# Storing the middle blocks row by row, with a load between the two rows, in a softmax-minus-one-hot kernel

## The chip, the cores and the metric

The kernel runs on one core of one Trainium2 chip. The metric is the device time of one execution in microseconds, lower is better; a time is the median of several runs. A microsecond is written us.

## The reference, cut to what matters

The input is 8192 rows (8 x 1024) of 8192 float32 numbers each, and one label for each row. The result is the gradient of the cross entropy: the softmax of each row, less 1 at the label's place.

```python
batch, seq_len, vocab = 8, 1024, 8192
logits_max = np.max(logits, axis=-1, keepdims=True)
exp_logits = np.exp(logits - logits_max)
softmax = exp_logits / np.sum(exp_logits, axis=-1, keepdims=True)
one_hot[batch_idx, seq_idx, labels] = 1.0
return (softmax - one_hot).astype(np.float32)
```

256 MiB are read and 256 MiB are written; nothing is read twice.

## The kernel before

**Tiles.** The 8192 rows are cut into B = 32 blocks of 256 rows. A block lies on 128 partitions with G = 2 rows to a partition, so it has 8 MiB; "row 0" and "row 1" of a block below mean the 128 first and the 128 second rows of the partitions, 4 MiB each. On chip there is one buffer `X` with SLOTS = 3 places for whole blocks; block b uses place b % 3. The work is done in place: the load writes into the place, the exponentials and the result overwrite it, and the store reads it. So block b can be loaded only when the store of block b-3 has landed.

**The work on one block** (`work(b)`). VectorE (DVE) takes the maximum of row 0 (`row_max`), ScalarE (ACT) makes its exponentials and their sum (`exponentials`), DVE takes the maximum of row 1, ACT makes its exponentials, and then DVE finishes row 0 and row 1 (`finish`): a reciprocal of the sum, and one `scalar_tensor_tensor` that multiplies the row by it and subtracts the mark at the label. The marks lie in PSUM as bytes (`hot`) and are made by ACT ahead of time (`mark`, two activations a row). `finished[t]` is what a store waits for, t = 2b or 2b+1.

**The transfers.** All loads and stores are issued by SyncE (SP), one after another in one order that is written out by hand; SP does nothing else. If an instruction of SP has to wait, all that stand behind it wait too. They all go into one hardware queue (q1), which works them off in their order on 16 DMA engines, each engine with its share of every transfer. `LOADS` and `STORES` say with one letter for each block how it is moved: `w` is the whole block in one transfer of 8 MiB, `r` is two transfers of 4 MiB, row 0 and row 1. A store by rows waits for its own row alone; a whole store waits for `finished` of row 1. Loads of blocks 0 to 5 and 31 go by rows, those of 6 to 30 whole. The last block is stored in four quarters.

**The order.** The loads of blocks 0, 1 and 2 come first. Then, after the work of block b, its store is issued, and behind it the load of the next block that has not been loaded. After block EARLY = 3 there is no load, so that from block 4 on the load behind the store of block b is that of b+2 and not b+3: it needs the place of block b-1. After block LATE = 27 two loads (29 and 30) follow, so that block 31 is loaded behind the store of block 28. In the middle the order of SP is: store of 10, load of 12, store of 11, load of 13, and so on.

Where this text writes S(b) it means the store of block b and S(b,0), S(b,1) its rows; L(b) is the load of block b.

Of the kernel before, what the change touches and what calls it, by code (L numbers as in the profile page):

```python
# [9 lines left out]
SLOTS = 3  # L10
EARLY = 3
LATE = 27

LOADS = "rrrrrrwwwwwwwwwwwwwwwwwwwwwwwwwr"
STORES = "rrrwwwwwwwwwwwwwwwwwwwwwwwwwrrrr"


@with_exitstack
def kernel(
# [19 lines left out]
    B = T // G  # L39
# [25 lines left out]
    with tc.tile_critical():  # L65
# [6 lines left out]
        def run(engine, waits, counter, method, **operands):  # L72

            waits = list(dict.fromkeys(waits))
            for w in waits[:-1]:
                engine.wait_ge(*w)
            instruction = getattr(engine, method)(**operands)  # L77
            for w in waits[-1:]:
                instruction._wait_ge(*w)
            step = 16 if method == "dma_start" else 1  # L80
            instruction.then_inc(counter, step)
            count[counter.name] = count.get(counter.name, 0) + step
            return counter, count[counter.name]
# [9 lines left out]
        def meets(a, b):  # L93
            sets = [[set(range(*d.indices(n))) for d, n in zip(p, (P, G))] for p in (a, b)]
            return all(x & y for x, y in zip(*sets))
# [4 lines left out]
        def load(b):  # L100
            loaded[b] = []
            before = stored.get(b - SLOTS, [])
            for q, piece in enumerate(PIECES[LOADS[b]]):
                ps, js = piece
                free = [w for other, w in before if meets(piece, other)]
                w = run(
                    nc.sync, free, got[b % SLOTS][q], "dma_start",
                    out=X[ps, b % SLOTS, js, :], in_=x_b[b, ps, js, :],
                )
                loaded[b].append((piece, w))  # L110

        def store(b):
            stored[b] = []
            if b == B - 1:
                for t in (T - G, T - 1):
                    j = t % G
                    for i, cs in enumerate(sides):
                        w = run(
                            nc.sync, [sides_done[t][i]], put[b % SLOTS][G * j + i],
                            "dma_start", out=o_b[b, every, one[j], cs], in_=X[every, b % SLOTS, one[j], cs],  # L120
                        )
                        stored[b].append(((every, one[j]), w))
                return
            for q, piece in enumerate(PIECES[STORES[b]]):
                ps, js = piece
                w = run(
                    nc.sync, [finished[b * G + js.stop - 1]], put[b % SLOTS][q], "dma_start",
                    out=o_b[b, ps, js, :], in_=X[ps, b % SLOTS, js, :],
                )
                stored[b].append((piece, w))  # L130
# [106 lines left out]
        def work(b):  # L237
            t0, t1 = b * G, b * G + 1
            row_max(t0)
            exponentials(t0)  # L240
            if b == 0:
                mark(0)
                mark(1)
            row_max(t1)
            exponentials(t1)
            finish(t0)
            mark(t0 + G)
            finish(t1)
            mark(t1 + G)

        nxt = SLOTS
        for b in range(B):
            work(b)
            store(b)
            if b == EARLY:
                continue
            for _ in range(2 if b == LATE else 1):
                if nxt < B:
                    load(nxt)
                    nxt += 1  # L260
        for b in range(B - SLOTS, B):
            for _, w in stored[b]:
                nc.scalar.wait_ge(*w)
# [30 lines left out]
```

## Time and profile before

| what | before |
|---|---|
| median of 3 runs | 1263.8 us (1263.55 to 1264.0) |
| the profiled execution, its own time | 1262.39 us |
| its span, first to last instruction | 1260.6 us |
| DVE busy | 1120.2 us (89%) |
| ACT busy | 722.7 us (57%) |
| bytes moved | 536.99 MB, mean 426 GB/s over the span |

The span is read from the hardware profiler's record of one execution; the execution's own time is 1.8 us more than its span, and the median of the runs is 1.4 us more than that. Every instruction is issued through one helper, so all have one line (L77): groups are told apart by what they write and read ("X<-in_logits_dram" is a load, "out_dram<-X" a store, "m<-X" the row maximum, "X<-X,r,hot" the finish). Rows of the timeline begin with the start in us and the duration in us, "x2" says that two instructions were merged into one row, and the bracket at the end gives the idle time before and what ended it. A DMA instruction on "SPq" shows when SP issued the transfer, not when the data moved. Rows of a table by windows hold, for each stretch, the busy time of each engine, the granted TensorE clock, the share of the DMA engines and the GB/s.

### The profile page before, as it was taken

To read this page: it belongs to the slowest core of one execution; us is meant where nothing else is said; L and a number is where in the kernel's file an instruction comes from. 1 tells how busy PE (TensorE), PEld (TensorE's weight loads), DVE (VectorE), ACT (ScalarE), POOL (GpSimd) and SP (SyncE) were. 2 spreads that over 40 slices of the span, in tenths; PEclk is the share of its full clock that TensorE was granted. 3 is DMA by queue.
4 is the path that set the end of the run, shared out by engine and by line. 5 is a ranking of instruction groups with operands and counts; after the bars stand their busy time and mean duration, and the time that the engine had idled before them with its cause. 6 is when DMAs were issued, how large, how long until landed. Compare 5 with 4: busy or idle time off the path is not lost.

```text
span 1260.6 us, 747 instructions
## 1 busy us (share of the span) xinstructions
PE 0.4 (0%) x2; PEld 0.3 (0%) x2; DVE 1120.2 (89%) x208; ACT 722.7 (57%) x257; POOL 2.3 (0%) x7
## 2 busy tenths in 40 slices
PE   0000000000000000000000000000000000000000
PEld 0000000000000000000000000000000000000000
DVE  6899999688988889888898888988889888898995
ACT  3666676356655575545755547555475554755662
POOL 0000000000000000000000000000000000000000
DMA  9999999999999999999999999999999999999998
GB/s 401 416 433 433 434 448 433 430 433 430 433 430 433 433 420 416 430 433 433 416 443 406 433 433 433 412 420 433 433 433 401 430 433 433 433 433 400 435 432 368
DMA packets 11574, 536.99 MB, mean 426 GB/s; under 512 B 1296, under 2 KB 1296, under 8 KB 1328
## 3 DMA queue, kind: packets, MB, share of 16 engines
q1 hardware_dynamic: 11520, 536.88, 99.5%
q10 hardware_dynamic: 48, 0.07, 0.0%
q14 instruction: 6, 0.05, 0.0%
HBM read 268.50 MB, written 268.44 MB: 426 GB/s over the span
## 4 chain that ended last, share of the span: by engine, by line
DVE 50%; DMA 43%; issue 4%; ACT 2%; SPq 0%
DMA X<-in_logits_dram 43%; DVE X L77 25%; DVE m L77 25%; ACT X L77 1%; DVE r L77 1%; ACT hot L77 0%; SPq L77 0%; ACT away L77 0%; SPq L289 0%; SPq L65 0%
## 5 line engine op out<-in xcount | busy, mean ns | idle before, releaser
L77 DVE TENSOR_REDUCE m<-X 128x1 f32<-128x8192 f32 x64 | 553.0, 8680 | 114.3 <-DMA X<-in_logits_dram 114.3
L77 ACT ACTIVATE X<-X,m 128x8192 f32<-128x8192 f32 x64 | 455.8, 7122 | 308.6 <-DVE m L77 308.6
L77 DVE SCALAR_TENSOR_TENSOR X<-X,r,hot 128x8192 f32<-128x8192 f32 (+1 forms) x66 | 560.1, 8489 | 3.8 <-ACT hot L77 1.6
L77 ACT ACTIVATE away<-count,word 128x2048 bf16<-128x2048 int16 x64 | 128.1, 2001 | 199.1 <-DVE X L77 148.1
L77 ACT ACTIVATE hot<-away,unit,minus 128x2048 int32<-128x2048 bf16 x64 | 131.9, 2061 | 2.1
L77 DVE RECIPROCAL r<-s 128x1 f32<-128x1 f32 x64 | 9.9, 155 | 2.4 <-ACT X L77 2.4
L77 ACT ACTIVATION_READ_ACCUMULATOR X<-X,m 128x1 f32 x64 | 11.9, 186 | 0.0
L77 DVE CAST lab_f<-lab_raw 32x256 f32<-32x256 int32 x1 | 0.4, 372 | 4.9 <-DMA lab_raw<-in_labels_dram 4.9
L77 ACT ACT_TABLE_LOAD x1 | 1.3, 1283 | 3.2 <-POOL count L77 3.2
L77 POOL IOTA count<- 128x2048 int16 x1 | 1.8, 1823 | 0.0
L77 DVE TENSOR_TENSOR unit<-unit,part 128x64 f32<-128x64 f32 x3 | 0.7, 224 | 0.1
L77 DVE CAST lab<-hot 128x64 int32<-128x64 f32 x1 | 0.2, 225 | 0.5 <-PE hot L77 0.5
L77 DVE TENSOR_SCALAR part<-minus 128x64 f32<-128x64 f32 x3 | 0.6, 195 | 0.1
L77 PE MATMUL hot<-ident,lab_f 32*128 32x32 f32 x2 | 0.4, 302 | 5.3 <-DVE lab_f L77 5.3
L77 PEld LDWEIGHTS hot<-ident,lab_f 32*128 32x128 f32 x2 | 0.3, 196 | 5.3 <-DVE lab_f L77 5.3
L77 DVE TENSOR_SCALAR part<-lab 128x64 int32<-128x64 int32 x1 | 0.2, 196 | 0.0
L77 DVE TENSOR_SCALAR word<-part 128x64 f32<-128x64 int32 x1 | 0.2, 195 | 0.0
L77 DVE TENSOR_SCALAR lab<-lab 128x64 int32<-128x64 int32 x1 | 0.2, 195 | 0.0
L77 DVE CAST minus<-lab 128x64 f32<-128x64 int32 x1 | 0.2, 195 | 0.0
L77 DVE TENSOR_SCALAR unit<-minus 128x64 f32<-128x64 f32 x1 | 0.2, 195 | 0.0
L77 DVE TENSOR_SCALAR minus<-unit 128x64 f32<-128x64 f32 x1 | 0.2, 195 | 0.0
L77 POOL TENSOR_SCALAR_AFFINE_SELECT ident<-ident 32x32 f32<-32x32 f32 x1 | 0.2, 203 | 0.1
(5 smaller groups left out, 0.5 us busy)
## 6 DMA issues: line engine op xcount, KB each, us to landing
X<-in_logits_dram SPq DMA_DIRECT2D x14, 4096.0 KB, 19.4
out_dram<-X SPq DMA_DIRECT2D x12, 4096.0 KB, 29.5
out_dram<-X SPq DMA_DIRECT2D x4, 2048.0 KB, 12.2
out_dram<-X SPq DMA_DIRECT2D x25, 23.7
X<-in_logits_dram SPq DMA_DIRECT2D x25, 43.1
lab_raw<-in_labels_dram ACTq DMA_DIRECT2D x1, 64.0 KB, 4.0
```

Of the source, the lines that this page charges most:

```text
L77: instruction = getattr(engine, method)(**operands)
```

## The change

The middle blocks are stored by rows as well, and the load of block b+2 is issued between the two rows of block b, for b from 4 to 27. After block 27 one more load (30) follows the store. What each engine computes, and its order, stays.

```diff
-STORES = "rrrwwwwwwwwwwwwwwwwwwwwwwwwwrrrr"
+STORES = "rrrrrrrrrrrrrrrrrrrrrrrrrrrrrrrr"
...
-        def store(b):
+        def store(b, between):
             stored[b] = []
...
             for q, piece in enumerate(PIECES[STORES[b]]):
                 ps, js = piece
+                if js.start:
+                    between()
                 w = run(
                     nc.sync, [finished[b * G + js.stop - 1]], put[b % SLOTS][q], "dma_start",
                     out=o_b[b, ps, js, :], in_=X[ps, b % SLOTS, js, :],
                 )
...
-        nxt = SLOTS
+        ahead = iter(range(SLOTS, B))
+
+        def next_load():
+            for n in ahead:
+                load(n)
+                return
+
         for b in range(B):
             work(b)
-            store(b)
-            if b == EARLY:
-                continue
-            for _ in range(2 if b == LATE else 1):
-                if nxt < B:
-                    load(nxt)
-                    nxt += 1
+            middle = EARLY < b <= LATE
+            store(b, next_load if middle else lambda: None)
+            if b < EARLY or b >= LATE:
+                next_load()
```

In the changed kernel the order of SP in the middle is: S(10,0), L(12), S(10,1), S(11,0), L(13), S(11,1), and so on. Up to the load of block 5 nothing moves. Block 3 is stored by rows with no load behind it. At the end the order is S(27,0), L(29), S(27,1), L(30), S(28,0), S(28,1), and from there on as before.

## The prediction

> **What bounds the kernel now.** I read the page first: busy times, the 40 slices, the chain that ended last.
>
> ```profile
> span 1260.6 us, 747 instructions
> ...
> DVE  6899999688988889888898888988889888898995
> ...
> DMA  9999999999999999999999999999999999999998
> GB/s 401 416 433 433 434 448 433 430 433 430 433 430 433 433 420 416 430 433 433 416 443 406 433 433 433 412 420 433 433 433 401 430 433 433 433 433 400 435 432 368
> ...
> DVE 50%; DMA 43%; issue 4%; ACT 2%; SPq 0%
> ```
>
> DVE carries half of the chain and is busy most of the time, but the DMA engines are busy in every slice, the first too. The chain as a list, one cycle of the middle, and the DVE timeline of that block show how the two meet:
>
> ```profile
> 276.78 16.00 DVE m L77 x2
> ...
> 311.80 0.33 SPq L77
> 312.13 0.04 issue
> 312.18 42.87 DMA X<-in_logits_dram
> 355.08 16.00 DVE m L77 x2
> ```
>
> ```profile
> 294.17 8.75 DVE L77 SCALAR_TENSOR_TENSOR X<-X,r,hot 128x8192 f32<-128x8192 f32 x1
> ```
>
> A block starts on DVE when its load lands (276.78). Row 0 is finished at 294.17 + 8.75 = 302.92, 26.1 us later; the whole block at 311.80, 35.0 us later. Then its store and the load of two blocks on are issued. The table of waits for the middle (230 to 1142 us) says that DVE is the one that waits:
>
> ```profile
> DVE m L77 <- DMA X<-in_logits_dram: 108.7, 24, 10.1
> ```
>
> 108.7 us over 24 loads: 35 us of work in a cycle of more than 39. So DMA sets the pace, and the question is whether its engines move bytes as fast as they can. SP's timeline gives the cycle in two stretches:
>
> ```profile
> 72.27 10.57 SPq L77 DMA_DIRECT2D X<-in_logits_dram  x2
> ...
> 111.19 10.47 SPq L77 DMA_DIRECT2D X<-in_logits_dram  x2
> ...
> 150.29 10.24 SPq L77 DMA_DIRECT2D X<-in_logits_dram  x2
> ...
> 273.17 0.33 SPq L77 DMA_DIRECT2D out_dram<-X  x1
> ...
> 1098.40 0.33 SPq L77 DMA_DIRECT2D out_dram<-X  x1
> 1098.78 23.30 SPq L77 DMA_DIRECT2D X<-in_logits_dram  x2
> ```
>
> Early, L(3,0), L(4,0) and L(5,0) are issued when S(0,0), S(1,0) and S(2,0) have landed: two cycles of 16.8 MB in 150.29 - 72.27 = 78.02 us, 39.01 each, all in transfers of one row. In the middle, from S(6) at 273.17 to S(27) at 1098.40, 21 cycles take 825.23 us, 39.30 each, all in whole blocks. The stretch with the smaller transfers is the faster one by 0.29 us a cycle. The table by windows, whose counts of whole packets are rougher, points the same way (last column):
>
> ```profile
> 72.27:150.29 78.02, 0.00 (x0) 0.00 (x0) 77.84 (x15) 51.64 (x19) 0.00 (x0) 1.00 1.00 431
> 390.09:1098.40 708.31, 0.00 (x0) 0.00 (x0) 628.50 (x108) 405.98 (x144) 0.00 (x0) 1.00 1.00 426
> 1162.00:1254.00 92.00, 0.00 (x0) 0.00 (x0) 84.33 (x17) 49.11 (x18) 0.00 (x0) 1.00 1.00 431
> ```
>
> 431 GB/s at both ends of the kernel, where transfers go by rows, 426 in the long middle. What differs besides the size is how much still lies in the queue when a store joins it. Issue to landing of the stores, middle and early:
>
> ```profile
> L77 SPq DMA_DIRECT2D out_dram<-X x22: 332/332/333, 273.2 to 1098.4; - x22
> ...
> DMA to landing us min/median/max: 22.9/23.6/24.6
> ```
>
> ```profile
> L77 SPq DMA_DIRECT2D out_dram<-X x5: 344/431/432, 82.9 to 160.6; - x5
> ...
> DMA to landing us min/median/max: 28.3/32.8/38.3
> ```
>
> A whole store moves in about 39.01 / 2 = 19.5 us, so in the middle it had 3.4 to 5.1 us between its issue and its first byte, the time of starting and landing included. What starting and landing cost on an empty queue the first load of the kernel shows:
>
> ```profile
> 0.96 12.42 DMA X<-in_logits_dram
> ```
>
> 12.42 us for one row, against 39.01 / 4 = 9.75 of moving: 2.7. That leaves the queue 0.7 to 2.4 us from dry whenever a middle store joins it, and the engines do not finish their shares at the same moment, so those ahead are already short of work. Early, a row's store (9.75) took at least 28.3: 18 us lay ahead of it. I read the 0.29 us a cycle as the price of the store that comes just in time.
>
> **The change part by part.**
>
> *The store of row 0 comes earlier.* Call D the landing of L(b). S(b,0) waits for row 0 alone, D + 26.1. In the queue stand then L(b+1), which lands a cycle after L(b), at D + 39.0, and S(b-1,1) behind it, to D + 48.8. So S(b,0) has 22 us ahead of it where S(b) had 4.
>
> *The load between.* L(b+2) needs the place of block b-1, so SP waits until S(b-1,1) has landed, D + 48.8. Behind the waiting SP stands S(b,1), whose row is ready at D + 35.0: it is held back 14 us, but its turn in the queue is only after L(b+2), so nobody feels that. Who covers the wait is S(b,0): 9.75 us, less the 2.7 of landing and starting, about 7 us left. Were this cover gone, each cycle would lose up to 2.7. So the thinnest point of the queue goes from 0.7 to 2.4 us to about 7, and the cycle, by the early rows, from 39.30 to 39.01. Those early cycles have the same pattern (a load that waits for a row's store, one row's transfer as cover). The rate itself has a bound: L(31,0) and L(31,1) are issued on the landing of S(28,0) and S(28,1),
>
> ```profile
> 1172.12 10.01 SPq L77 DMA_DIRECT2D X<-in_logits_dram  x2
> ```
>
> and the merged row ends with the second issue (0.34 us), so one row's landing follows the other by 9.67 us: 38.7 a cycle with no loss at all. The gain per cycle lies between nothing and 0.6; I take 0.29. It is had by the cycles with L(6) to L(29), 24 of them: 24 x 0.29 = 7.0 us.
>
> *25 more transfers.* Stores of blocks 3 to 27 become two. On SP that is 25 issues of 0.33 us, hidden because SP only waits in between. In the queue the cost of a transfer's ends is in the 39.01 already, which has four transfers a cycle where the changed middle has three.
>
> *L(30).* Before, it was issued when S(27) had landed, with L(29) as its cover:
>
> ```profile
> 1121.74 0.34 SPq L77 DMA_DIRECT2D X<-in_logits_dram  x1
> ```
>
> Now S(27,1) stands directly before it, and L(30) waits for that very store. Nothing lies in the queue meanwhile; S(28,0) and S(28,1) stand behind SP's wait. The queue runs dry once: between 0.4 (SP's own 0.33 and 0.04 in the chain) and 2.7 us. I take 2.0, nearer to the first load, because landing and starting both lie bare here.
>
> *The start and the end.* L(6) stands before S(4,1) now and lands 9.75 us sooner:
>
> ```profile
> 238.16 17.28 DVE L77 TENSOR_REDUCE m<-X 128x1 f32<-128x8192 f32 x2 [10.11 <-DMA X<-in_logits_dram]
> ...
> 1237.64 8.87 DVE L77 SCALAR_TENSOR_TENSOR X<-X,r,hot 128x4096 f32<-128x4096 f32 x2
> ```
>
> The idle 10.11 us of DVE nearly goes, and DVE runs about 10 us ahead of before all the way, still waiting some 4 us a cycle. That buys nothing at the end: DVE is done at 1246.5, and 14.1 us are left to the end of the span, of which the last quarter (a quarter of 19.5) moves for 4.9. The rest is starting, landing and a backlog of stores: the queue ends the kernel, and DVE only gets further ahead of it.
>
> **Sum:** -7.0 + 2.0 = -5.0 us. The profiled time 1262.4 becomes 1257.4, and the median, which lies 1.4 above it, 1258.8.
>
> **The rivals.**
>
> *The loss stays.* The 0.29 us might belong to something else that the middle has and the ends have not (whole loads, engines drifting apart over a long run). Then the cycle stays at 39.30 and the dry queue at L(30) is added: 1263.8 + 2.0 = 1265.8. For it: only two early cycles stand against 21. Against it: the tail window also shows 431.
>
> *The turn from a whole load to a row's store costs (slower).* The trace has this turn once, L(30) before S(28,0). From L(30)'s issue to L(31,0)'s, that is from S(27) landed to S(28,0) landed, L(29), L(30) and S(28,0) move: 1172.12 - 1121.74 = 50.38 us for 21 MB, where 39.01 a cycle would give 48.8. 1.6 us are lost with a queue that is far from dry. The changed kernel makes this turn in each of the 24 cycles. If the 1.6 belongs to the turn, the cycle is 40.6: 24 x 1.3 + 2.0 = 33, 1297 us. It decides from 0.2 us a turn on (24 x 0.2 eats the forecast's 5.0). Against it: it is one event, and the early turns from a load's row to a store's row are inside 39.01.
>
> *Each transfer has a fixed price.* More transfers of half the size would each pay for their own landing and start, at most 2.7: 25 x 2.7 = 68, 1331 us. The tail's 9.67 us from row to row, against 9.75 by the early cycles, leaves no such price while others are queued, so I give this little. The Trainium skill, DMA: Bandwidth & Descriptors, section "Anatomy of one DMA", fits 2.0 us plus the bytes for each DMA issued from GpSimd; an estimate from that figure for 25 more would be +50 us. By the 9.67 this trace does not agree for queued transfers; for the one at the bare L(30) it does.
>
> *It doesn't do what it says:* out, since SP's order in the program is the one described; only how early SP can issue L(b+2) is open, and S(b,0) covers 7 us of that.
>
> **How the numbers follow.** Forecast 0.58, loss stays 0.24, the turn 0.14, fixed price 0.02, other mishaps 0.02. Runs of this kernel can be told apart by about 0.2%, 2.5 us: faster is below 1261.3, slower above 1266.3. The forecast is faster throughout (0.58); the loss that stays falls within for 0.18 and, with the dearer end of L(30), above for 0.06; the rest is slower, 0.24 in all. Low end: all loss gone, 24 x (39.30 - 38.68) = 14.9, less 2.0: 1250.9, taken as 1251. High end: loss stays, L(30) at 2.7 and 0.1 a cycle for more turns (2.4): 1268.9, taken as 1269. The turn at 1.6 and the fixed price are left out, with what little lies outside otherwise.
>
> **What would show it.** Right: loads in the middle issued 39.0 us apart; middle row stores landing well over 25 us after issue (S(b,0): 9.75 + 22); DVE's wait before block 6 almost gone and its other waits near 4 us; L(30) issued when S(27,1) lands, and one dip in GB/s there. Wrong: a cycle of 39.3 or more although stores join a deep queue (the loss was not lateness), or a cycle above 40 (the turn).

## The result and the profile after

| what | before | changed kernel |
|---|---|---|
| median of 5 runs | 1263.65 us (1263.42 to 1264.0) | 1257.26 us (1256.21 to 1257.93) |
| ratio to before, 95% interval | | 0.9949 (0.9934 to 0.9963) |
| the profiled execution, its own time | 1262.39 us | 1257.26 us |
| its span | 1260.6 us | 1255.5 us |
| load to load in the middle | 39.30 us | 38.91 us |

The change gains 0.5%, 6.4 us between the medians and 5.1 between the two profiled executions (that of before lay 1.3 us under its median). The page of the changed kernel, the same lines as of before:

```profile
span 1255.5 us, 797 instructions
...
DVE  6899999988998889988889888898888988889991
...
DMA  9999999999999999999999999999999999998999
GB/s 403 418 434 432 431 429 437 432 424 430 434 438 428 427 431 434 438 428 431 426 433 445 435 433 423 433 439 440 432 421 433 436 443 434 431 400 357 433 429 390
...
DMA 80%; DVE 14%; ACT 2%; issue 1%; SPq 1%
DMA out_dram<-X 77%; DVE X L77 7%; DVE m L77 7%; DMA X<-in_logits_dram 3%; ACT X L77 1%; SPq L77 1%; ACT hot L77 0%; ACT away L77 0%; DVE r L77 0%; SPq L294 0%; SPq L65 0%
```

Busy times are what they were. The chain (of work that ended last) has changed: it was half DVE, and now four fifths of it are DMA, nearly all of it the landing of stores, because SP waits for a row's store to land before each load. DMA is still busy in every slice, but GB/s has a hole in the 37th (357).

SP's timeline: the issue of L(5), of five whole loads of the middle, and of L(31). Each of the whole loads is issued when row 1 of the block three before it has been stored:

```profile
150.71 10.11 SPq L77 DMA_DIRECT2D X<-in_logits_dram  x2
...
238.75 0.34 SPq L77 DMA_DIRECT2D X<-in_logits_dram  x1
...
553.10 0.34 SPq L77 DMA_DIRECT2D X<-in_logits_dram  x1
...
669.14 0.34 SPq L77 DMA_DIRECT2D X<-in_logits_dram  x1
...
1094.79 0.34 SPq L77 DMA_DIRECT2D X<-in_logits_dram  x1
...
1133.45 0.34 SPq L77 DMA_DIRECT2D X<-in_logits_dram  x1
...
1166.49 10.18 SPq L77 DMA_DIRECT2D X<-in_logits_dram  x2
```

From L(7) at 238.75 to L(29) at 1094.79 there are 22 cycles of 38.91 us. But they are not alike: the first eight, to 553.10, take 39.29 on average, as long as before; the last fourteen take 38.69, which is the pace with no loss at all (four times the 9.67 of one row's landing after another). L(30) is issued at 1133.45, and S(28,0) has landed at 1166.49: 33.0 us for L(30) and one row's store, which at 38.69 a cycle take 29.0. 4.0 us are lost there, against 2.0 for the same turn before (50.4 us for the five rows from L(29) to S(28,0), less 48.4). The table by windows shows that the queue runs dry there (last two columns: DMA share, GB/s):

```profile
1110.00:1120.00 10.00, 0.00 (x0) 0.00 (x0) 9.96 (x3) 4.06 (x2) 0.00 (x0) 1.00 1.02 442
1120.00:1130.00 10.00, 0.00 (x0) 0.00 (x0) 6.30 (x2) 4.06 (x2) 0.00 (x0) 1.00 0.80 344
1130.00:1140.00 10.00, 0.00 (x0) 0.00 (x0) 10.00 (x2) 7.21 (x2) 0.00 (x0) 1.00 0.64 249
```

Stores of the middle, issue to landing:

```profile
L77 SPq DMA_DIRECT2D out_dram<-X x47: 332/572/993, 199.9 to 1095.2; - x47
...
DMA to landing us min/median/max: 29.0/37.9/39.5
```

At least 29.0 us for a row that moves in 9.7: the queue is deep when a store joins it. And DVE, block 6, the end of its work, and its waits for loads over the whole run:

```profile
229.07 17.28 DVE L77 TENSOR_REDUCE m<-X 128x1 f32<-128x8192 f32 x2 [0.84 <-DMA X<-in_logits_dram]
```

```profile
1219.91 8.87 DVE L77 SCALAR_TENSOR_TENSOR X<-X,r,hot 128x4096 f32<-128x4096 f32 x2
```

```profile
DVE m L77 <- DMA X<-in_logits_dram: 94.0, 26, 5.0
```

Its wait before block 6 has gone from 10.11 to 0.84 us and the rest stay at some 4; it is done at 1228.8, 17.7 us sooner than before and 26.7 us ahead of the end. Nothing of that reaches the end.

### The profile page after: what moved, and what is told of

Read it like the earlier page. It is cut to its first block, busy times and chain, and to the rows that moved or that the text cites. A ratio compares the mean times of both kernels' runs of the same rounds, so it can differ in the third digit from the quotient of the medians.

```text
span 1255.5 us, 797 instructions
## 1 busy us (share of the span) xinstructions
PE 0.4 (0%) x2; PEld 0.3 (0%) x2; DVE 1120.2 (89%) x208; ACT 722.7 (58%) x257; POOL 2.3 (0%) x7
## 4 chain that ended last, share of the span: by engine, by line
DMA 80%; DVE 14%; ACT 2%; issue 1%; SPq 1%
DMA out_dram<-X 77%; DVE X L77 7%; DVE m L77 7%; DMA X<-in_logits_dram 3%; ACT X L77 1%; SPq L77 1%; ACT hot L77 0%; ACT away L77 0%; DVE r L77 0%; SPq L294 0%; SPq L65 0%
```

## The experiments

Two theories were open. **Late store**: the loss of the middle comes from a store that joins a nearly dry queue. **Size**: one-row transfers are faster by themselves. A third question was whether the load between the rows is what helps. The first four kernels ran on one chip, beside 15 runs of the kernel before with a median of 1263.21 us.

### rows_only: rows, but no load between

```diff
 (the kernel before)
-STORES = "rrrwwwwwwwwwwwwwwwwwwwwwwwwwrrrr"
+STORES = "rrrrrrrrrrrrrrrrrrrrrrrrrrrrrrrr"
```

> The kernel before with all stores by rows, and no load between the rows: S(b,0), S(b,1), L(b+2). S(b,0) waits for row 0 alone and joins the queue about 13 us before it is needed. Late-store theory (the loss of the middle is the store that arrives when the queue is nearly dry): the gain does not need the load between, so the cycle between loads falls from 39.30 us to 38.9 or less as in the changed kernel, L(30) keeps its cover, and the time is 1252 to 1256 us, below the changed kernel's 1257.3. Rival (the load between the rows is what fills the queue): no gain, 1262 to 1265 us.

1252.93 us (1251.98 to 1254.1), ratio to before 0.9917 (0.9903 to 0.9930). Its first and last load of the middle on SP, and the landing of its stores:

```profile
273.68 0.44 SPq L77 DMA_DIRECT2D X<-in_logits_dram  x1
...
1092.89 22.92 SPq L77 DMA_DIRECT2D X<-in_logits_dram  x2
```

```profile
DMA to landing us min/median/max: 22.2/23.0/24.2
```

21 cycles of 39.01 us. A row takes 22.2 us or more, of which it moves for 9.7, so some 10 to 12 us of other transfers lie ahead of it. The gain is there, and is larger than the change's: no load between is needed. L(30) follows L(29) here, and no queue runs dry.

### rows_late: rows, as late as before

```diff
 (rows_only)
                 ps, js = piece
+                last_row = G if EARLY <= b <= LATE else js.stop
                 w = run(
-                    nc.sync, [finished[b * G + js.stop - 1]], put[b % SLOTS][q], "dma_start",
+                    nc.sync, [finished[b * G + last_row - 1]], put[b % SLOTS][q], "dma_start",
```

> As rows_only, but for blocks 4 to 27 (and 3) both rows' stores wait until row 1 is finished, as the whole store did: transfers of 4 MiB that come as late as before. Late-store theory: the loss stays, cycle 39.3 us or a little more, 1263 to 1267 us. Rival (transfers of one row are faster by themselves, early or late): 1252 to 1257 us.

1265.01 us (1263.56 to 1267.12), ratio 1.0015 (1.0006 to 1.0024).

```profile
274.24 0.78 SPq L77 DMA_DIRECT2D X<-in_logits_dram  x1
...
1101.92 23.45 SPq L77 DMA_DIRECT2D X<-in_logits_dram  x2
```

```profile
DMA to landing us min/median/max: 13.3/18.9/24.5
```

39.41 us a cycle. The quickest landing, 13.3, is the first row's: 3.6 us more than its moving, of which the start and the landing on an empty queue are 2.7. Small transfers that come late lose as much as whole ones. Size by itself gains nothing; the transfer more in each cycle costs about 0.1 us.

### whole_early: whole blocks, but sooner

```diff
 (the kernel before)
-            for i, c in enumerate(sides if t >= T - G else [slice(0, V)]):
+            short = t % G == 1 and EARLY < t // G <= LATE
+            for i, c in enumerate(sides if t >= T - G else [slice(0, V // 8 if short else V)]):
```

> The kernel before with whole stores and its order, but VectorE finishes only the first eighth of row 1 in blocks 4 to 27 (the rest of that row is left as exponentials), so that the whole store comes 7.6 us sooner after the load than before. Late-store theory: cycle 38.7 to 39.0 us with whole blocks as well, 1252 to 1258 us. Rival (size): cycle 39.3 us, 1261 to 1264 us, VectorE only waits longer.

1251.36 us (1249.32 to 1254.14), ratio 0.9905 (0.9891 to 0.9920).

```profile
265.29 0.43 SPq L77 DMA_DIRECT2D X<-in_logits_dram  x1
...
694.41 0.43 SPq L77 DMA_DIRECT2D X<-in_logits_dram  x1
...
1084.93 30.94 SPq L77 DMA_DIRECT2D X<-in_logits_dram  x2
```

```profile
DMA to landing us min/median/max: 30.4/30.7/31.7
```

39.03 us a cycle, with the transfers, the order and the waits of the kernel before. The kernel leaves seven eighths of each second row of blocks 4 to 27 unfinished, so its result is not the gradient; it is there for its time, and DVE is done some 7.6 us sooner with each block (seven eighths of 8.75). Its stores land 30.4 to 31.7 us after issue instead of 22.9 to 24.6. That DVE also works less is a second difference, but rows_only leaves nothing out and gains as much. Together with rows_late this settles late store against size, each way round.

### end_covered: cover for L(30)

```diff
 (the changed kernel)
-LATE = 27
+LATE = 28
```

> The changed kernel with one constant more (LATE 28): block 28 also has its load between its rows, so the end runs S(27,0), L(29), S(27,1), S(28,0), L(30), S(28,1), L(31,0), L(31,1), and L(30) waits for S(27,1) with S(28,0) in the queue. Theory: the dry queue at L(30) costs the slowest engine 2.3 us and puts all engines in step, after which 1.9 us more are lost at the end of L(30); both go, 1253 us. Rival (the 1.9 us belong to the turn from load 30 to a store and not to the dry queue): 1255 us.

1253.55 us (1252.65 to 1254.2), ratio 0.9919 (0.9906 to 0.9933), against 0.9949 of the changed kernel: 0.3%, 3.7 us between the medians.

```profile
277.42 0.34 SPq L77 DMA_DIRECT2D X<-in_logits_dram  x1
...
668.67 0.34 SPq L77 DMA_DIRECT2D X<-in_logits_dram  x1
...
1095.80 0.34 SPq L77 DMA_DIRECT2D X<-in_logits_dram  x1
...
1134.46 0.34 SPq L77 DMA_DIRECT2D X<-in_logits_dram  x1
...
1144.13 29.34 SPq L77 DMA_DIRECT2D X<-in_logits_dram  x2
```

```profile
1120.00:1140.00 20.00, 0.00 (x0) 0.00 (x0) 16.32 (x3) 10.57 (x3) 0.00 (x0) 1.00 0.99 429
1140.00:1160.00 20.00, 0.00 (x0) 0.00 (x0) 19.69 (x5) 12.13 (x7) 0.00 (x0) 1.00 1.02 441
```

L(30) is issued at 1134.46, S(28,0) has landed and L(31,0) is issued at 1144.13, 9.67 us later; the hole in the GB/s is gone, and the cycles (38.96 over the 22 from L(8) at 277.42 to L(30)) are on average those of the changed kernel. So the dry queue at L(30) cost the change over a third of what it could have gained. With the end mended, the order with a load between the rows and the one without it (rows_only, 0.9917) are the same.

### dry_once: why the cycles get shorter

What let the changed kernel's cycles fall from 39.29 to 38.69 in the middle of the run? The packet records of the trace show when each of the 16 DMA engines closes its share of a transfer: sixteen packets of 4 bytes end each one. The time from the first of them to the last, called the spread below, in us:

| closing near (us) | 100 | 300 | 390 | 550 | 900 | 1130 | 1157 |
|---|---|---|---|---|---|---|---|
| before | 0.5 | 1.3 | 2.5 | 3.1 | 3.1 | 2.4 | 3.3 |
| changed kernel | 1.0 | 3.6 | 4.6 | 6.3 | 6.0 | 6.0 | 0.9 |

In the changed kernel the engines drift apart up to 550 us, and from there on the cycle is 38.69; the dry queue at L(30) gathers them. Before, they stay within 3.3. That suggested: engines in step lose time at the turn from a load to a store, spread engines do not. (In the changed kernel's first eight cycles the last packet of a load takes longer on many engines, up to 3.6 us instead of 2.42; other packets hardly ever do.) The test puts one dry queue into the middle of end_covered:

```diff
 (end_covered, in load)
                 free = [w for other, w in before if meets(piece, other)]
+                if b == 17:
+                    free = free + [w for _, w in stored[15]]
```

> The kernel end_covered with one wait more, in the middle: L(17) also waits until S(15,0) has landed, which lies directly before it in the queue, so the queue runs dry once, at about 640 us. In-step theory (engines that work side by side at the same pace lose time at the turn from a load to a store, and lose less as they drift apart): the dry queue puts all engines in step again, so beside its own 2 to 3 us the cycles behind it go back from 38.7 to about 39.2 us for some eight of them: 5 to 8 us above end_covered's 1253.6, 1258 to 1261 us. Rival (the cycles get shorter late in the run for another reason): only the dry queue itself, 1255.5 to 1257 us, and cycles of 38.7 behind it.

1261.64 us (1260.02 to 1263.0), ratio 0.9984 (0.9975 to 0.9993); this kernel and the three behind it ran on another chip, where before took 1262.89. That is 0.65% or 8 us above end_covered, slightly more than the 1261 expected at most.

```profile
238.00 0.34 SPq L77 DMA_DIRECT2D X<-in_logits_dram  x1
...
590.46 0.34 SPq L77 DMA_DIRECT2D X<-in_logits_dram  x1
...
638.82 0.34 SPq L77 DMA_DIRECT2D X<-in_logits_dram  x1
...
671.60 0.34 SPq L77 DMA_DIRECT2D X<-in_logits_dram  x1
...
1103.25 0.34 SPq L77 DMA_DIRECT2D X<-in_logits_dram  x1
```

```profile
630.00:640.00 10.00, 0.00 (x0) 0.00 (x0) 9.96 (x3) 8.62 (x3) 0.00 (x0) 1.00 0.64 262
```

L(17) is issued at 638.82 behind the dry queue. From L(16) to L(18), two cycles, 81.1 us go by, 2.8 more than two of the 39.16 that the nine cycles ahead of it took. The eleven cycles behind it, L(18) to L(29), take 39.24 each; in end_covered the same eleven (668.67 to 1095.80) take 38.83. So the dry queue costs some 3 us by itself and 4.5 through what follows. In the records the spread is 4.2 us ahead of it, 0.7 behind it, and 6 again at 1090. With early stores, then, engines in step cost time, and a reason that only lies late in the run is out. How far apart they are does not alone set the loss: in whole_early the spread is 1.2 to 2.6 us over the eleven cycles from 265.29 to 694.41, and these take 39.01.

### stagger_end, stagger_rows, stagger_before: spreading the engines by hand

```diff
 (end_covered, rows_only and the kernel before)
-LOADS = "rrrrrrwwwwwwwwwwwwwwwwwwwwwwwwwr"
+LOADS = "rrsrrrwwwwwwwwwwwwwwwwwwwwwwwwwr"
...
+        cuts = (0, 96, 110, 120, 126, 128)
+        PIECES["s"] = [(every, one[0])] + [(slice(a, z), one[1]) for a, z in zip(cuts, cuts[1:])]
```

> The kernel end_covered with row 1 of block 2 loaded in five pieces of 96, 14, 10, 6 and 2 partitions instead of one of 128, so that the DMA engines get between 6 and 10 rows of it instead of 8 each: the same bytes, the slowest engine has 2 rows (2.4 us) more, and the engines are spread over 4.8 us from 60 us on. In-step theory: the cycles are near 38.7 us from the start instead of 39.0 on average, 24 x 0.3 = 7 us less, 2.4 more: 1247 to 1251 us. Rival (spread does not matter): 1256 us.

1266.75 us (1266.52 to 1267.81), ratio 1.0025 (1.0014 to 1.0035): nearly 16 us above the highest time expected. SP's loads L(3,0), L(7) and L(29), and the stretch in which the pieces move:

```profile
90.85 10.01 SPq L77 DMA_DIRECT2D X<-in_logits_dram  x2
...
256.29 0.34 SPq L77 DMA_DIRECT2D X<-in_logits_dram  x1
...
1108.49 0.34 SPq L77 DMA_DIRECT2D X<-in_logits_dram  x1
```

```profile
40.00:50.00 10.00, 0.00 (x0) 0.00 (x0) 7.53 (x3) 8.69 (x4) 0.00 (x0) 1.00 0.97 419
50.00:60.00 10.00, 0.00 (x0) 0.00 (x0) 10.00 (x2) 4.06 (x2) 0.00 (x0) 1.00 1.08 262
60.00:70.00 10.00, 0.00 (x0) 0.00 (x0) 10.00 (x2) 7.21 (x2) 0.00 (x0) 1.00 1.08 203
70.00:80.00 10.00, 0.00 (x0) 0.00 (x0) 9.93 (x5) 7.36 (x3) 0.00 (x0) 1.00 0.86 279
```

The cycles are what was expected: 22 of 38.74 us, from L(7) on. The spread in the records is 6 us from 120 us on. But the five pieces moved at 203 to 279 GB/s for 30 us, and L(3,0) is issued at 90.85, where the changed kernel has 72.51: 18 us are lost before anything is won, and the shorter cycles win back some 5 of them (span 1266.0 us against 1252.4 of end_covered). In the records a one-row packet of the 96 partitions takes mostly 2.2 to 2.6 us instead of 1.21, and some of the smaller pieces take up to 4.3. The Trainium skill, DMA: Bandwidth & Descriptors, section "The descriptor swizzle", has each engine write to one port of its own in a transfer to 128 partitions. That the pieces made engines share ports would fit the doubled packets, but no run here separates it.

> The same five pieces in the kernel rows_only. In-step theory: 1247 to 1251 us, and whichever of the two orders wins by more than a microsecond shows whether the load between the rows is worth anything. Rival: 1255 us.

1267.22 us (1265.66 to 1273.13), ratio 1.0044 (1.0028 to 1.0059). The same: 21 cycles of 38.75 us from L(8) to L(29), where rows_only had 39.01, and the same loss at the pieces (L(3,0) at 90.78). It is above the 1251 us expected at most by as much, and as the two orders are 0.5 us apart, neither is shown to be the better one.

```profile
291.48 0.79 SPq L77 DMA_DIRECT2D X<-in_logits_dram  x1
...
1105.32 22.93 SPq L77 DMA_DIRECT2D X<-in_logits_dram  x2
```

> The same five pieces in the kernel before, whose whole stores come late. Theory: a late store lets the engines that are ahead wait for it, which gathers them again within a few cycles, so the cycles stay at 39.3 us and the time is 1262 to 1266 us. Rival (spread alone is enough, whenever the store comes): 1255 to 1259 us.

1283.53 us (1281.74 to 1284.74), ratio 1.0156 (1.0143 to 1.0169).

```profile
291.86 0.43 SPq L77 DMA_DIRECT2D X<-in_logits_dram  x1
...
1119.31 0.42 SPq L77 DMA_DIRECT2D X<-in_logits_dram  x1
```

With late whole stores the 21 cycles stay at 39.40 us in spite of the spread at the start: 18 us and more lost at the pieces and nothing won, so that the time is far above the 1266 expected at most. The late store takes the spread away again: in the records it is 6.8 us when L(7) lands and 3.1 when L(8) does.

## Why the prediction was right, point by point

**DMA sets the pace, and a store that comes just in time costs the middle.** Right, and shown: rows_late keeps the size and loses the gain, whole_early keeps whole blocks and gets it.

**What the lateness does** was put as a queue short of work, with the engines that are ahead short of it first. That step is not borne out. In the kernel before, the 21 cycles lose 13.0 us against 38.68 a cycle, and the packet records leave only 1.6 us in which an engine is idle (this and the next figures are means of the 16 engines). Most of the loss, 7.6 us, lies in the last packets of the stores, which take longer than others of their size; 1.2 lie in the last packets of loads, 2.2 in other packets. In rows_late the last packets of the stores again have 7.7. In rows_only, in whole_early and in the first eight cycles of the changed kernel they have less than 0.1, and what is lost lies in the last packets of loads (3.1, 5.7 and 1.7). So a store that comes early ends the loss at its own end, and not at the end of the loads, which goes on until the engines have drifted apart. Why the last packets of a late store take longer, no run here shows.

**The cycle: 39.01 predicted, 38.91 measured**, from two early row-by-row cycles. The size was right by luck. Those rows were cycles in step, and the changed kernel's first eight were slower still, 39.29 behind a deep queue, all but the 39.3 that the prediction had named as a sign of being wrong; the last fourteen, at the bound of 38.7, made up for it. From S(2,0)'s landing (150.29 before, 150.71 now) to L(29)'s (1141.47 before; 1133.45 now, where S(27,1) has landed behind it as well, so that the bytes are the same) the change gains 8.4 us, where 7.0 were forecast. DVE shows the landing of L(29) before:

```profile
1141.47 17.28 DVE L77 TENSOR_REDUCE m<-X 128x1 f32<-128x8192 f32 x2 [4.04 <-DMA X<-in_logits_dram]
```

**L(30): +2.0 predicted.** From there to the end of the span before takes 119.1 us and the changed kernel 122.05: +2.9. The engines were 6 us apart, those ahead were idle until the last one was done, and then all stood in step (a spread of 0.9 us) for the turn behind it. With 0.4 us more at the start the sum is -8.4 + 2.9 + 0.4 = -5.1 us of span, where -5.0 was forecast. Both terms were too small, by 1.4 and 0.9 us, and with opposite signs, so that the sum is closer than its terms; that too is luck.

**S(b,0) as cover, S(b,1) held back unfelt.** Right: nothing runs dry in the middle, and the landings of 29.0 to 39.5 us are about the 9.75 + 22 of the prediction for row 0, and 9.75 + 29 for row 1, which has S(b,0) and L(b+2) ahead of it. But the load between the rows, which made that cover needed, gains nothing: rows_only has no such order and is at least as fast.

**25 more transfers at no price.** Nearly: rows_late bounds it at 0.1 us each. The rival of a fixed price, 1331 us, is out. The Trainium skill, DMA: Bandwidth & Descriptors, section "Anatomy of one DMA", fits 2.0 us and the bytes for a DMA issued from GpSimd; for one more transfer in a full queue issued from SP these 0.1 us do not agree with such a price. Nor had the prediction a measurement for saying that the trace agrees at the bare L(30): the kernel before has no such load, and around that of the changed kernel 4.0 us are lost.

**The rival of the turn** had the right place, not the right law. In the changed kernel the loss does sit where a load gives way to a store, but it ends when the engines are some 6 us apart: near 0.6 us a cycle for the first eight and nothing for the last fourteen, not 1.6 each time. And the rival of the loss that stays had named engines that drift apart as a cause; here the cycles without loss are those of the engines that have drifted.

**Start and end of DVE.** Right: 10.11 to 0.84 us, and nothing at the end.

## What to carry to other kernels

When DMA is the bound, look not only at whether the engines are busy but at how much is queued when a transfer joins: issue to landing, less the moving time, less a start on an empty queue. If one or two microseconds are left, issue the transfer in parts as they become ready; that alone was worth 0.8% here. And see that no load's wait is for the transfer directly ahead of it: one such place cost 0.3%.

## What the runs showed of the hardware

That 16 DMA engines, all busy, move less when they are in step than when they are 6 us apart (39.0 to 39.3 against 38.7 us for 16.8 MB) was not expected. Nor that a store that joins late would have slow last packets although hardly an engine is idle, or that a transfer to 96 partitions, and smaller ones behind it, would run at 203 to 279 GB/s instead of some 430. Why the last packets take longer, of a late store or of a load with the engines in step, and whether a cheaper spread would bring the 1253 us down further, stays open. The fastest kernels that leave nothing out are rows_only and end_covered, both 0.8% faster than before.
